# Query and gating-unit input blocks computed as two seven-product pairs, their rows kept in DRAM

## The chip, the cores and the metric

One core of a Trainium2 chip runs the kernel. Its engines are TensorE (PE: matmuls, with PEld for the loading of its stationary operand), VectorE (DVE), ScalarE (ACT), GpSimd (POOL) and SyncE (SP); each takes its instructions in order. SP, ACT and POOL also issue the DMA transfers. The metric is device time in microseconds, the median of several runs. Three runs of the kernel before took 1492.59, 1493.43 and 1494.11 us.

## The reference

Two layers of a bidirectional encoder over 512 positions and 2048 features, everything in float32:

```python
def hybrid_layer(x, ...):
    h = rms_norm(x, norm_w)
    proj = jnp.einsum('bsd,de->bse', h, w_in)          # 2048 -> 6144 columns
    q, k, v, g_attn, c_in, c_b, c_c, g_conv, s_u, s_v, g_sgu = split(proj)
    o_attn = attention_branch(q, k, v, ...)            # per-head rms norm of q and k, axial rope,
                                                       # 8 query heads on 2 key/value heads
    o_conv = short_conv_branch(c_in, c_b, c_c, conv_w) # c_b * conv3(c_c * c_in)
    o_sgu = sgu_branch(s_u, s_v, ...)                  # gelu(u) * (W_s norm(gelu(v)) + b), 4 groups of 128
    mixed = concatenate([rms_norm(o) * silu(gate) for each branch])
    return x + jnp.einsum('bse,ed->bsd', mixed, w_out) # 2048 -> 2048
```

A last RMS norm follows the second layer.

## The kernel before, in words

The input projection has twelve blocks of 512 columns. Block 0 holds k and v, 1 and 2 the queries, 3 and 4 the attention's gate, 5 to 8 the convolution, 9 to 11 the gating unit's v, its u and its gate. Each block is one `product` (L201): 16 feature tiles of 128, four accumulators of 128x512. Float32 accuracy comes from splitting each operand into a high and a low part and summing three matmuls, so that a product has 16 x 4 x 3 = 192 matmuls. Weights arrive in pairs of tiles (`load_pair`, L75, three buffers `wr`, issued by SP); `weight_parts` (L195) makes the two parts: ACT casts the high one (`wH`, L98), DVE subtracts to get the low one (`wL`, L99), five buffers each. The RMS norm's per-feature weight is multiplied into x when x is split; its per-position factor `rx` is applied when a product's rows leave the accumulators.

A layer runs block 0, then blocks 1 and 2 (`qblock`, L388: rows scaled by `rx`, `rope_rows` at L295 for norm and rope, then a 32x32 block transpose on DVE with a trip through DRAM to turn them), then attention per head (`scores` L347, `values` L372) with the convolution's blocks 5 to 8. Then come block 9 and the norm of gelu(v) (L453 to L467: gelu, square, reduce, four scaled multiplies, split into `vnH` and `vnL`), block 10, the gating matmuls (L477 to L479), block 11, and the gates 3 and 4 (`gates`, L500).

The output projection is already done in fewer multiplications: two calls of `pair` (L588), each of which computes two 512-column blocks as one 2x2 block product in seven products of 48 matmuls instead of eight (Winograd's form of Strassen's scheme). Its operands are halves and sums of halves of the mixed rows (A11 to N4), its weights running sums (X, Y), some of them formed by accumulating DMA transfers on POOL's queue (L596, L632). Between the layers, rows of the result go to DRAM (`Rows`), and `arrive` (L726) reads them back transposed, scales them on ACT (L733) and splits them into the next layer's operands.

A tile scheduler sets the order of instructions on each engine from the program's order, its dependences and the number of buffers per tag; a buffer comes free when its last reader is done. `mA`, `kv`, `qa`, `qb` and `o` are tags of large tiles, `t`, `qr` and `p` tags of 128x512 tiles with four buffers each. `acc` (4), `sc` (3) and `ps` (1) are the eight accumulator banks.

Of the kernel before, what the change touches and what calls it, by code (L numbers as in the profile page):

```python
# [8 lines left out]
F32 = mybir.dt.float32  # L9
# [5 lines left out]
P = 128  # L15
D = 2048
S = 512
# [16 lines left out]
def trunk_kernel(ctx: ExitStack, tc: tile.TileContext, xT, xn, win, wout, wcols, convw, qkw, sgun,  # L34
# [15 lines left out]
    def nm(s):  # L50
        uid[0] += 1
        return f"{s}_{uid[0]}"
# [84 lines left out]
    class Transposer:  # L137
# [27 lines left out]
        def get(self, t):  # L165
            return self.e[:, t]

    def by_block(ap):
        return ap.rearrange("p (s a i) -> p s a i", a=4, i=32)

# [50 lines left out]

    sqx = Squares()

    xraw = [big.tile([P, 4, S], F32, tag="mA", name=f"xraw{i}", bufs=4) for i in range(4)]
    first = []

    def load_x(k, n):
# [33 lines left out]
    for l in range(L):  # L261
# [6 lines left out]
        else:  # L268
            acc = product(win[l, 0], False, kps=kps, then=late)
            Rx = broadcast_x(rx)  # L270

        cos = lay.tile([P, ST, HD], F32, tag="swH", name=nm("cos"))
        sin = lay.tile([P, ST, HD], F32, tag="swL", name=nm("sin"))
        nc.sync.dma_start(out=cos, in_=rope[:, 0])
# [8 lines left out]
        nc.sync.dma_start(out=sb, in_=sgub[l])  # L283


        def rows_out(ps, st, n, on_act):
            q = T("qr")
            c = rx[:, st:st + 1]
            if on_act:
                nc.scalar.activation(q[:, :n], ps[:, :n], AF.Copy, scale=c)  # L290
            else:
                nc.vector.tensor_scalar(out=q[:, :n], in0=ps[:, :n], scalar1=c, scalar2=None, op0=ALU.mult)
            return q

        def rope_rows(q, st, nh, w):  # L295
            n = nh * HD
            qv = q[:, :n]
            t2 = T()
            nc.scalar.activation(t2[:, :n], qv, AF.Square)
# [3 lines left out]
            rq = rstd(ss, nh, 1.0 / HD)  # L303
            t1 = T()
# [16 lines left out]
        def transposed(rows, n, dst):  # L321
            tr = Transposer(n, "mA", 4)
            for st in range(ST):
                tr.put(st, rows[st][:, :n * HD])
            tr.move()
            for h in range(n):
                split(by_block(dst[h][0]), by_block(dst[h][1]), tr.get(h))
            return dst

        krows, vt = [], []  # L330
        for st in range(ST):
            krows.append(rows_out(acc[st], st, 256, True))
            v = T()
            nc.vector.tensor_scalar(out=v[:, :256], in0=acc[st][:, 256:], scalar1=rx[:, st:st + 1], scalar2=None,
                                    op0=ALU.mult)
            vt.append(v)
        vT = big.tile([P, ST, S], F32R, tag="kv", name=nm("vT"), bufs=2)
        kTt = big.tile([P, 2 * NKV, S], F32R, tag="kv", name=nm("kT"), bufs=2)
        for st in range(ST):
            split(vT[:, st, :256], vT[:, st, 256:], vt[st][:, :256])  # L340
        for st in range(ST):
            rope_rows(krows[st], st, NKV, qw[:, 1])
        kT = transposed(krows, NKV, [(kTt[:, 2 * h], kTt[:, 2 * h + 1]) for h in range(NKV)])

        oat = []

# [38 lines left out]
            nc.scalar.copy(o, po)  # L385
            oat.append(o)

        def qblock(b):  # L388
            acc = product(win[l, 1 + b], False)
            rows = [rows_out(acc[st], st, S, st % 2 == 0) for st in range(ST)]  # L390
            for st in range(ST):
                rope_rows(rows[st], st, 4, qw[:, 0])
            tag = "qa" if b == 0 else "qb"
            return transposed(rows, 4, [[big.tile([P, S], F32R, tag=tag, name=nm(tag), bufs=8) for _ in range(2)]
                                        for _ in range(4)])

        qs = qblock(0) + qblock(1)
        prev = None
        for h in range(NQ):
            cur = scores(h, qs[h])  # L400
# [70 lines left out]
        for st in range(ST):  # L471
# [17 lines left out]
        acc = product(win[l, 11], False)  # L489
        tr = Transposer(4, "mA", 4)  # L490
        for st in range(ST):
            g = T("qr")
            nc.scalar.activation(g, acc[st], AF.Silu, scale=rx[:, st:st + 1])
# [190 lines left out]
        if not last:  # L684
            out_rows = {}
            xH, xL = [None] * KT, [None] * KT

            class Rows:


                def __init__(self, spare):
                    self.spare = spare
                    self.m = dram.tile([P, 4, ST, 4 * 32], F32, tag="mv", name=nm("mv"), bufs=6)
                    self.got = 0

                def put(self, st, rows):
                    if self.got == 0 and self.spare:
                        self.both = big.tile([P, 2, 4, 2, 4, 32], F32, tag="mA", name=nm("blk"), bufs=4)
                    if self.got % 2 == 0:
                        if self.spare:  # L700
                            self.d = self.both[:, self.got // 2]
                        else:
                            self.d = big.tile([P, 4, 2, 4, 32], F32, tag="o", name=nm("blk"), bufs=2)
                    nc.vector.transpose(out=self.d[:, :, st % 2].rearrange("p b t i -> p t b i"),
                                        in_=rows.rearrange("p (t b j) -> p t b j", b=4, j=32))
                    self.got += 1
                    if self.got % 2 == 0:
                        nc.scalar.dma_start(out=self.m[:, :, st - 1:st + 1],
                                            in_=self.d.rearrange("p b s t i -> p b s (t i)"))

                def back(self):
                    e = big.tile([P, 4, ST * 4 * 32], F32, tag="mA", name=nm("rearr"), bufs=4)
                    mv = self.m.rearrange("(a j) b s f -> b j a (s f)", a=4)
                    for b in range(4):
                        nc.sync.dma_start(out=e[32 * b:32 * b + 32], in_=mv[b])
                    return e.rearrange("p a (s t i) -> p t s a i", s=ST, t=4)

            def complete(b, st, junk):
                c = C[b, st]
                squares(b, st, junk)  # L720
                nc.sync.dma_start(out=x1d[b, st], in_=c)
                if b not in out_rows:
                    out_rows[b] = Rows(b == 0)
                out_rows[b].put(st, c)

            def arrive(b):  # L726
                e_ = out_rows[b].back()
# [121 lines left out]
```

## Time and profile before

| | |
|---|---|
| median of three runs | 1493.43 us (1492.59 to 1494.11) |
| profiled execution | 1494.47 us, span 1492.7 us |
| mean granted clock of TensorE | 0.992 of full speed |
| PE busy | 1462.6 us (98%), 6422 matmuls |
| DVE busy | 972.4 us (65%), 1854 instructions |
| ACT busy | 681.3 us (46%), 1253 instructions |
| POOL busy | 112.3 us (8%), 120 instructions |
| HBM read, written | 186.96 MB, 36.70 MB |

The span is the time from the first to the last instruction of the profiled execution; the rest of its time lies around it. Matmuls are pipelined, so that one has a duration of about 0.39 us in the rows while the next starts 0.23 us after it. The page's chain of work that ended last gives PE 90% of the span and DMA 6%.

### The profile page before, as it was taken

To read this page: it belongs to the slowest core of one execution; us is meant where nothing else is said; L and a number is where in the kernel's file an instruction comes from. 1 tells how busy PE (TensorE), PEld (TensorE's weight loads), DVE (VectorE), ACT (ScalarE), POOL (GpSimd) and SP (SyncE) were. 2 spreads that over 40 slices of the span, in tenths; PEclk is the share of its full clock that TensorE was granted. 3 is DMA by queue.
4 is the path that set the end of the run, shared out by engine and by line. 5 is a ranking of instruction groups with operands and counts; after the bars stand their busy time and mean duration, and the time that the engine had idled before them with its cause. 6 is when DMAs were issued, how large, how long until landed. Compare 5 with 4: busy or idle time off the path is not lost.

```text
span 1492.7 us, 18358 instructions
## 1 busy us (share of the span) xinstructions
PE 1462.6 (98%) x6422; PEld 1205.5 (81%) x6422; DVE 972.4 (65%) x1854; ACT 681.3 (46%) x1253; POOL 112.3 (8%) x120
## 2 busy tenths in 40 slices
PE   9999999999999999997989999999999999999997
PEld 7888888888888888876868888888888888888785
DVE  7657898645553467875846578986455534678676
ACT  7333365533332446555643343565333334465553
POOL 0110000000011001111000100000000110011110
PEclk9999999999999999998999999999999999999999
DMA  7344577623337634697664345776232376346963
GB/s 277 102 114 141 181 217 225 184 86 99 92 101 210 202 96 101 141 328 179 178 165 128 113 141 173 222 217 192 85 99 92 99 209 194 106 100 143 251 139 130
DMA packets 78909, 233.25 MB, mean 156 GB/s; under 512 B 9184, under 2 KB 14560, under 8 KB 76000
## 3 DMA queue, kind: packets, MB, share of 16 engines
q1 hardware_dynamic: 65088, 202.68, 43.8%
q0 software_dynamic: 9216, 25.17, 9.3%
q10 hardware_dynamic: 4512, 4.23, 0.8%
q8 instruction: 50, 0.82, 0.2%
q14 instruction: 43, 0.35, 0.1%
HBM read 186.96 MB, written 36.70 MB: 150 GB/s over the span
## 4 chain that ended last, share of the span: by engine, by line
PE 90%; DMA 6%; DVE 1%; ACT 1%; SPq 1%; issue 0%; ACTq 0%; POOLq 0%
PE acc L218 59%; PE sc L218 9%; PE acc L611 3%; PE acc L612 3%; PE acc L613 3%; PE sc L613 2%; PE sc L611 2%; PE sc L612 2%; DMA mv<-blk 2%; DMA rearr<-mv 2%; PE ps L381 1%; PE ps L382 1%; PE ps L383 1%; PE sc L357 1%; PE sc L355 1%; PE sc L356 1%
## 5 line engine op out<-in xcount | busy, mean ns | idle before, releaser
L99 DVE TENSOR_TENSOR wL<-wr,wH 128x512 fp32r<-128x512 f32 x448 | 304.0, 685 | 355.1 <-ACT wH L98 325.5
L98 ACT CAST wH<-wr 128x512 fp32r<-128x512 f32 x448 | 275.9, 621 | 532.6 <-PE acc L218 390.6
L218 PE MATMUL acc<-x,wH 128*128 128x512 f32 x1408 | 436.8, 389 | 0.4 <-DVE qr L420 0.4
L218 PE MATMUL acc<-wH,x 128*128 128x512 f32 x1280 | 393.0, 391 | 7.6 <-ACT wH L98 7.6
L218 PEld LDWEIGHTS acc<-x,wH 128*128 128x128 f32 x1408 | 264.2, 188 | 55.6 <-DVE qr L420 0.8
L218 PEld LDWEIGHTS acc<-wH,x 128*128 128x128 f32 x1280 | 240.9, 189 | 59.6 <-ACT wH L98 9.5
L218 PE MATMUL acc<-x,wL 128*128 128x512 f32 x704 | 273.2, 389 | 0.0
L218 PE MATMUL acc<-wL,x 128*128 128x512 f32 x640 | 244.2, 390 | 0.0
L218 PEld LDWEIGHTS acc<-x,wL 128*128 128x128 f32 x704 | 132.2, 188 | 27.4
L218 PEld LDWEIGHTS acc<-wL,x 128*128 128x128 f32 x640 | 120.4, 188 | 25.4 <-DVE wL L99 0.4
L611 PE MATMUL acc<-wH,n 128*128 128x512 f32 x192 | 75.9, 395 | 7.5 <-ACT wH L98 7.5
L105 POOL TENSOR_TENSOR s<-s,negh 128x4 f32<-128x4 f32 (+2 forms) x44 | 52.3, 1190 | 369.7 <-DVE s L103 364.2
L218 PE MATMUL sc<-wH,x 128*128 128x512 f32 x256 | 78.8, 389 | 0.0
L612 PE MATMUL acc<-wH,n 128*128 128x512 f32 x192 | 75.7, 394 | 0.0
L99 DVE TENSOR_TENSOR wL<-wx,wH 128x512 fp32r<-128x512 f32 x88 | 57.7, 684 | 24.2 <-ACT wH L98 18.7
L98 ACT CAST wH<-wx 128x512 fp32r<-128x512 f32 x88 | 52.8, 619 | 36.9 <-PE acc L218 11.9
L364 ACT ACTIVATE p<-sc,sa 128x512 f32<-128x512 f32 x64 | 44.1, 689 | 54.4 <-DVE sa L361 37.2
L613 PE MATMUL acc<-wL,n 128*128 128x512 f32 x192 | 66.1, 394 | 0.0
L218 PEld LDWEIGHTS sc<-wH,x 128*128 128x128 f32 x256 | 48.1, 188 | 10.0
L218 PE MATMUL sc<-wL,x 128*128 128x512 f32 x128 | 49.8, 389 | 0.0
L98 ACT CAST wH<-wy 128x512 fp32r<-128x512 f32 x64 | 38.9, 622 | 23.2 <-PE sc L612 12.8
L611 PEld LDWEIGHTS acc<-wH,n 128*128 128x128 f32 x192 | 36.6, 191 | 15.6 <-ACT wH L98 7.9
(231 smaller groups left out, 1963.7 us busy)
## 6 DMA issues: line engine op xcount, KB each, us to landing
wr<-in_win SPq DMA_DIRECT2D x191, 512.0 KB, 3.6
rearr<-mv SPq DMA_DIRECT2D x104, 256.0 KB, 5.4
mv<-blk SPq DMA_DIRECT2D x22, 1024.0 KB, 4.7
wr<-in_wout SPq DMA_DIRECT2D x32, 512.0 KB, 5.4
wy<-in_wout SPq DMA_DIRECT2D x16, 512.0 KB, 5.2
wy<-in_wout POOLq DMA_DIRECT2D x16, 512.0 KB, 9.2
wx<-in_wout SPq DMA_DIRECT2D x16, 512.0 KB, 8.3
wx<-wy POOLq DMA_DIRECT2D x16, 512.0 KB, 5.0
```

What stands on the lines that cost most here:

```text
L98: nc.scalar.copy(H, src)
L99: nc.vector.tensor_tensor(out=Lo, in0=src, in1=f32(H), op=ALU.subtract)
L105: nc.gpsimd.tensor_tensor(out=r, in0=v, in1=negh[:, :n], op=ALU.pow)
L218: nc.tensor.matmul(acc[e], a, b, start=(kp == kps[0] and j == 0 and i == 0), stop=(kp == kps[-1] and j == 1 and i == 2))
L355: nc.tensor.matmul(sc, qH[:, ss], kH, start=True, stop=False)
L356: nc.tensor.matmul(sc, qH[:, ss], kL, start=False, stop=False)
L357: nc.tensor.matmul(sc, qL[:, ss], kH, start=False, stop=True)
L364: nc.scalar.activation(p, sc, AF.Exp, scale=SCALE, bias=nm_, accum_out=su)
L381: nc.tensor.matmul(po, a, pH[:, t], start=(t == 0), stop=False)
L611: nc.tensor.matmul(bank[t], a, H, start=(k == 0 and p not in (6, 4)), stop=False, skip_group_check=True)
L612: nc.tensor.matmul(bank[t], c, H, start=False, stop=False, skip_group_check=True)
L613: nc.tensor.matmul(bank[t], a, Lo, start=False, stop=(k == 7), skip_group_check=True)
```

## The change

Blocks 1 and 2, and blocks 10 and 11, are each computed as a pair of seven products (`early_pair`), right behind block 0 and ahead of attention. The order is p = 1, 7, 5, 3, 6, 2, 4. Operands are the halves of the existing xH and xL, and four new sums of halves (E1 to E4) that `difference` builds for eight pairs of feature tiles: two scaled copies on ACT, four half-width adds on DVE, two splits. Weight sums are kept in four X tiles (tag `kv`, two buffers); at p=7 each weight tile gets X added to it in turn: X += w on DVE, then w += the second block's lower half by an accumulating transfer on POOL. For its last quarter w is a pair of 128x512 tiles (`spare`) instead of a `wr` buffer. q rows are roped with `rx` folded in and go through `Rows` to DRAM, as do the k rows; v rows, gelu(u) and silu(gate) go to DRAM as they are, and are read back where they are used. In layer 0 two of the raw x tiles move to the tag `kv`. In layer 1 `difference` works on rows that `arrive` kept, two of which are read again from DRAM. In the output projection the x1d stores go from SP's queue to POOL's, and the two `arrive` calls come behind p=5 and p=2 instead of p=3 and p=6.

```diff
+        def difference(k, i, lo, hi, shape=lambda ap: ap):
+            t0, t8 = T(), T()
+            nc.scalar.activation(shape(t0), lo, AF.Copy, scale=wc[:, 0, k:k + 1])
+            nc.scalar.activation(shape(t8), hi, AF.Copy, scale=wc[:, 0, 8 + k:9 + k])
+            nc.vector.tensor_tensor(out=t8[:, HALF:], in0=t0[:, HALF:], in1=t8[:, HALF:], op=ALU.subtract)
...
+            for (a, b), src, (h, lo_) in (((E2, E3), t0, tiles_[:2]), ((E4, E1), t8, tiles_[2:])):
+                split(h, lo_, src)
...
+        def early_pair(b0, b1, tags, complete):
+            s0, s1 = win[l, b0], win[l, b1]
+            wx = [big.tile([P, 2, 2, S], F32, tag="kv", name=nm("wx"), bufs=2) for _ in range(2)]
+            X = [wx[i // 2][:, i % 2] for i in range(4)]
+            for i in range(4):
+                nc.sync.dma_start(out=X[i], in_=s0[i])
...
+            for p in (1, 7, 5, 3, 6, 2, 4):
...
+                    if p == 7:
+                        if i < 3:
+                            w = load_pair(s1[i])
+                            nc.vector.tensor_tensor(out=X[i], in0=X[i], in1=w, op=ALU.add)
+                            nc.gpsimd.dma_start(out=w, in_=s1[4 + i], accum_op=ALU.add)
+                            w = [w[:, 0], w[:, 1]]
+                        else:
+                            w = spare
+                            for j in range(2):
+                                nc.sync.dma_start(out=w[j], in_=s1[i][:, j])
+                                nc.vector.tensor_tensor(out=X[i][:, j], in0=X[i][:, j], in1=w[j], op=ALU.add)
+                                nc.gpsimd.dma_start(out=w[j], in_=s1[4 + i][:, j], accum_op=ALU.add)
+                    elif p in (3, 2):
+                        w = load_pair((s1 if p == 3 else s0)[4 + i])
+                        nc.vector.tensor_tensor(out=X[i], in0=X[i], in1=w, op=ALU.add)
...
+        early_pair(1, 2, (("p", "p"), ("qr", "qr"), ("qr", "qr"), ("p", "sq")), q_rows)
+        early_pair(10, 11, (("qr", "qr"), ("qr", "qr"), ("p", "p"), ("p", "sq")), sgu_row)
...
-        acc = product(win[l, 10], False)
         gu = big.tile([P, ST, S], F32, tag="mA", name=nm("gu"), bufs=4)
-        for st in range(ST):
-            nc.scalar.activation(gu[:, st], acc[st], AF.Gelu, scale=rx[:, st:st + 1])
+        nc.sync.dma_start(out=gu, in_=sgu_rows[10])
...
-                nc.sync.dma_start(out=x1d[b, st], in_=c)
+                nc.gpsimd.dma_start(out=x1d[b, st], in_=c)
...
-            pair(2, 3, C, complete, False, {3: lambda: arrive(1), 6: lambda: arrive(0)})
+            pair(2, 3, C, complete, False, {5: lambda: arrive(1), 2: lambda: arrive(0)})
```

The order of the instructions moves in three places. On ACT, behind block 0 of layer 0, the kernel before has the next product's casts (wr_668 and later are weights of block 1):

```order
L98 CAST wH_534<-wr_482 128x512
L98 CAST wH_670<-wr_668 128x512
L98 CAST wH_686<-wr_668 128x512
L98 CAST wH_704<-wr_702 128x512
L98 CAST wH_720<-wr_702 128x512
L290 ACTIVATE qr_562<-acc_164,rc_501 128x256
```

The changed kernel has there the copies from the raw x tiles and the casts of E parts (e), and then the first casts of X weights (wx_764):

```order
L306 ACTIVATE t_640<-xraw_141,wc_144 128x512
L307 ACTIVATE t_641<-xraw_143,wc_144 128x512
L98 CAST e_635<-t_627 128x512
L98 CAST e_635<-t_628 128x512
L306 ACTIVATE t_653<-xraw_141,wc_144 128x512
L98 CAST e_648<-t_640 128x512
L307 ACTIVATE t_654<-xraw_143,wc_144 128x512
L98 CAST e_648<-t_641 128x512
L349 ACTIVATE t_692<-qr_680 128x256
L98 CAST wH_784<-wx_764 128x512
```

The last copies from xraw now stand ahead of the first cast of the next product. On DVE, in the same stretch of layer 0, the kernel before ropes q rows (qr) between the low parts of one product's weights (L307 to L319 are steps of `rope_rows`, L145 the transpose):

```order
L99 TENSOR_TENSOR wL_1119<-wr_1116,wH_1118 128x512
L307 SCALAR_TENSOR_TENSOR t_956<-qr_940,s_954,qw_554 128x128 x4
L301 TENSOR_REDUCE s_967<-t_965 128x4
L313 TENSOR_TENSOR t_948<-t_956,sin_551 128x8x32 x2
L103 TENSOR_SCALAR s_969<-s_967 128x4
L317 TENSOR_TENSOR t_956<-t_956,cos_550 128x512
L319 TENSOR_TENSOR qr_940<-t_956,t_948 128x512
```

The changed kernel has at p=7 of the q pair the low parts of accumulated weights (wr_914), the half-width adds of the last quarter (wx_765 with the spare tiles qr_772 and qr_773), and between them the K rows' rope and transposes (qr_683, qr_686):

```order
L99 TENSOR_TENSOR wL_919<-wr_914,wH_918 128x512
L103 TENSOR_SCALAR s_730<-s_728 128x2
L371 TENSOR_TENSOR t_717<-t_717,cos_666 128x256
L99 TENSOR_TENSOR wL_929<-wr_914,wH_928 128x512
L433 TENSOR_TENSOR wx_765<-wx_765,qr_772 128x512
L373 TENSOR_TENSOR qr_683<-t_717,t_709 128x256
L361 SCALAR_TENSOR_TENSOR t_734<-qr_686,s_732,qw_670 128x128 x2
L184 STREAM_TRANSPOSE blk_707<-qr_683 128x2x4x32
```

The adds into X and the low parts that depend on transfers now share the queue with the rope. On PE, ahead of the gating matmuls of layer 0, the kernel before has 206 matmuls between the last one of block 9 and the first of the gating: those of block 10 and some of another product. The last of them and the first of the gating are:

```order
L218 MATMUL acc_4097<-wH_4119,x_108 128x512
L218 MATMUL acc_4097<-wH_4119,x_124 128x512
L218 MATMUL acc_4097<-wL_4120,x_108 128x512
L218 MATMUL acc_4098<-wH_4119,x_108 128x512
L218 MATMUL acc_4098<-wH_4119,x_124 128x512
L477 MATMUL sc_4049<-vnH_3702,swH_3422 128x512
L478 MATMUL sc_4049<-vnL_3703,swH_3422 128x512
```

The changed kernel has 15 there, of the gates' product (L247):

```order
L247 MATMUL acc_4735<-x_110,wH_4788 128x512
L247 MATMUL acc_4735<-x_126,wH_4788 128x512
L247 MATMUL acc_4735<-x_110,wL_4789 128x512
L247 MATMUL acc_4735<-x_111,wH_4806 128x512
L247 MATMUL acc_4735<-x_127,wH_4806 128x512
L247 MATMUL acc_4735<-x_111,wL_4807 128x512
L631 MATMUL sc_4659<-vnH_4591,swH_4311 128x512
L631 MATMUL sc_4664<-vnH_4591,swH_4311 128x512
```

Block 10's product no longer stands between block 9 and the gating. In all the order has 6188 rows on PE instead of 6380, 2002 on DVE instead of 1712, and 1301 on ACT instead of 1105.

## Rows read from the trace of the kernel before

**Rows 1.** Section 1 of the page: busy time, share, instructions
```profile
PE 1462.6 (98%) x6422; PEld 1205.5 (81%) x6422; DVE 972.4 (65%) x1854; ACT 681.3 (46%) x1253; POOL 112.3 (8%) x120
```

**Rows 2.** Chain that ended last, a long product: start, length, what
```profile
536.52 44.88 PE acc L218 x198
```

**Rows 3.** PE's waits: line, waited for: total us, times, longest
```profile
PE acc L611 <- ACT wH L98: 7.9, 2, 7.5
PE acc L218 <- ACT wH L98: 7.6, 3, 6.3
```

**Rows 4.** Chain that ended last, change of layers
```profile
664.80 15.24 DMA mv<-blk
...
680.94 0.43 SPq L715
...
681.41 5.68 DMA rearr<-mv
...
745.42 7.67 DMA rearr<-mv
```

**Rows 5.** By stretch: length, PE, PEld, DVE, ACT, POOL busy, PEclk, DMA, GB/s
```profile
583.00:643.00 60.00, 60.00 (x265) 49.43 (x265) 53.62 (x86) 36.38 (x68) 11.42 (x13) 1.00 0.65 156
680.00:690.00 10.00, 2.86 (x13) 2.04 (x11) 0.00 (x0) 2.80 (x5) 0.00 (x0) 0.75 0.48 108
690.00:694.00 4.00, 3.69 (x9) 2.92 (x10) 3.25 (x5) 3.30 (x7) 1.68 (x2) 0.50 0.73 167
756.00:760.00 4.00, 3.69 (x9) 2.91 (x10) 3.71 (x7) 4.00 (x10) 0.00 (x0) 0.50 0.17 66
```

**Rows 6.** DVE in order of time, two stretches: start, us, line, operation
```profile
411.68 1.13 DVE L465 SCALAR_TENSOR_TENSOR qr<-qr,s,sn 128x128 f32<-128x128 f32 x4
...
590.25 0.42 DVE L529 TENSOR_TENSOR t<-o,t 128x256 f32<-128x256 f32 x1
590.59 0.69 DVE L99 TENSOR_TENSOR lA<-o,hA 128x512 fp32r<-128x512 f32 x1
591.19 1.29 DVE L99 TENSOR_TENSOR wL<-wy,wH 128x512 fp32r<-128x512 f32 x2
...
595.14 1.22 DVE L634 TENSOR_TENSOR wy<-wx,wr 128x1024 f32<-128x1024 f32 x1
596.27 0.69 DVE L99 TENSOR_TENSOR n<-t,n 128x512 fp32r<-128x512 f32 x1
```

**Rows 7.** Groups by form: busy, mean ns | idle before
```profile
L98 ACT CAST wH<-wr 128x512 fp32r<-128x512 f32 x448 | 275.9, 621 | 532.6 <-PE acc L218 390.6 <-PE sc L218 60.3 <-PE acc L612 23.2
L733 ACT ACTIVATE t<-rearr,wc 128x512 f32<-128x512 f32 x16 | 10.6, 712 | 27.7 <-DMA rearr<-mv 27.4 <-DVE x L99 0.4
```

**Rows 8.** DMA issues: count, KB each, median us to landing
```profile
wr<-in_win SPq DMA_DIRECT2D x191, 512.0 KB, 3.6
...
wy<-in_wout POOLq DMA_DIRECT2D x16, 512.0 KB, 9.2
wx<-in_wout SPq DMA_DIRECT2D x16, 512.0 KB, 8.3
...
c<-in_xn POOLq DMA_DIRECT2D x10, 256.0 KB, 6.6
...
p<-in_xn POOLq DMA_DIRECT2D x6, 256.0 KB, 4.2
```

**Rows 9.** Line L596 alone: POOL's accumulating transfers of 512 KB
```profile
DMA to landing us min/median/max: 7.9/9.2/13.7
```

**Rows 10.** Gating chain: last matmul of block 9, last split of vnL
```profile
404.11 0.39 PE L218 MATMUL acc<-wL,x 128*128 128x512 f32 x1
...
422.06 0.69 DVE L99 TENSOR_TENSOR vnL<-qr,vnH 128x512 fp32r<-128x512 f32 x1
```

More of the change, by code (lines that the diff above doesn't have):

```diff
@@ L166, in get, with __init__, put, back @@
             return self.e[:, t]
+    class Rows:
+        def __init__(self, n, spare):
+            self.n, self.spare, self.got = n, spare, 0
+            self.m = dram.tile([P, 4, ST, n * 32], F32, tag="rows", name=nm("rows"), bufs=8)
+        def put(self, st, rows):
+            n = self.n
+            if self.got == 0 and self.spare:
+                self.both = big.tile([P, 2, 4, 2, n, 32], F32, tag="mA", name=nm("blk"), bufs=4)
+            if self.got % 2 == 0:
+                if self.spare:
+                    self.d = self.both[:, self.got // 2]
+                else:
+                    self.d = big.tile([P, 4, 2, n, 32], F32, tag="o", name=nm("blk"), bufs=2)
+            nc.vector.transpose(out=self.d[:, :, st % 2].rearrange("p b t i -> p t b i"),
+                                in_=rows.rearrange("p (t b j) -> p t b j", b=4, j=32))
+            self.got += 1
+            if self.got % 2 == 0:
+                nc.scalar.dma_start(out=self.m[:, :, st - 1:st + 1], in_=self.d.rearrange("p b s t i -> p b s (t i)"))
+        def back(self, tag, bufs):
+            e = big.tile([P, 4, ST * self.n * 32], F32, tag=tag, name=nm("rearr"), bufs=bufs)
+            mv = self.m.rearrange("(a j) b s f -> b j a (s f)", a=4)
+            for b in range(4):
+                nc.sync.dma_start(out=e[32 * b:32 * b + 32], in_=mv[b])
+            return e.rearrange("p a (s t i) -> p t s a i", s=ST, t=self.n)
     def by_block(ap):
@@ L222, in trunk_kernel @@
     sqx = Squares()
-    xraw = [big.tile([P, 4, S], F32, tag="mA", name=f"xraw{i}", bufs=4) for i in range(4)]
+    xraw = [big.tile([P, 4, S], F32, tag="kv" if i % 2 else "mA", name=f"xraw{i}", bufs=2 if i % 2 else 4)
+            for i in range(4)]
     first = []
@@ L283, in trunk_kernel, with rope_rows @@
         nc.sync.dma_start(out=sb, in_=sgub[l])
[L286 to L295, printed above, removed]
+        def rope_rows(q, st, nh, w, scale=None):
             n = nh * HD
@@ L303, in rope_rows @@
             rq = rstd(ss, nh, 1.0 / HD)
+            if scale is not None:
+                rs_ = small(nh)
+                nc.vector.tensor_scalar(out=rs_, in0=rq, scalar1=scale, scalar2=None, op0=ALU.mult)
+                rq = rs_
             t1 = T()
@@ L319, in rope_rows @@
             nc.vector.tensor_tensor(out=qv, in0=t1[:, :n], in1=t2[:, :n], op=ALU.add)
-        def transposed(rows, n, dst):
-            tr = Transposer(n, "mA", 4)
-            for st in range(ST):
[L324 to L330, printed above, removed]
-        for st in range(ST):
[L332 to L336, printed above, removed]
+        krows = Rows(NKV, False)
@@ new lines, in trunk_kernel @@
+        vrows = dram.tile([P, ST, 256], F32, tag="vrows", name=nm("vrows"), bufs=2)
+        kv_rows = []
+        for st in range(ST):
+            q = T("qr")
+            nc.scalar.activation(q, acc[st], AF.Copy, scale=rx[:, st:st + 1])
+            nc.sync.dma_start(out=vrows[:, st], in_=q[:, 256:])
+            kv_rows.append(q)
+        for st in range(ST):
+            rope_rows(kv_rows[st], st, NKV, qw[:, 1])
+            krows.put(st, kv_rows[st][:, :256])
+        operand_x = {1: [(xH[k][:, :HALF], xL[k][:, :HALF]) for k in range(8)],
+                     2: [(xH[8 + k][:, :HALF], xL[8 + k][:, :HALF]) for k in range(8)],
+                     4: [(xH[8 + k][:, HALF:], xL[8 + k][:, HALF:]) for k in range(8)],
+                     5: E1, 6: E2, 7: E3, 3: E4}
@@ new lines, in trunk_kernel, with q_rows, sgu_row @@
+        qrows = {b: Rows(4, False) for b in (1, 2)}
+        def q_rows(b, st, c):
+            rope_rows(c, st, 4, qw[:, 0], rx[:, st:st + 1])
+            qrows[b].put(st, c)
+        sgu_rows = {b: dram.tile([P, ST, S], F32, tag=f"sgu{b}", name=nm("sgu"), bufs=2) for b in (10, 11)}
+        def sgu_row(b, st, c):
+            nc.scalar.activation(c, c, AF.Gelu if b == 10 else AF.Silu, scale=rx[:, st:st + 1])
+            nc.sync.dma_start(out=sgu_rows[b][:, st], in_=c)
+        early_pair(1, 2, (("p", "p"), ("qr", "qr"), ("qr", "qr"), ("p", "sq")), q_rows)
@@ L337, in trunk_kernel @@
+        early_pair(10, 11, (("qr", "qr"), ("qr", "qr"), ("p", "p"), ("p", "sq")), sgu_row)
         vT = big.tile([P, ST, S], F32R, tag="kv", name=nm("vT"), bufs=2)
         kTt = big.tile([P, 2 * NKV, S], F32R, tag="kv", name=nm("kT"), bufs=2)
+        kT = [(kTt[:, 2 * h], kTt[:, 2 * h + 1]) for h in range(NKV)]
+        e_ = krows.back("mA", 4)
+        for h in range(NKV):
+            split(by_block(kT[h][0]), by_block(kT[h][1]), e_[:, h])
         for st in range(ST):
[L340 removed]
@@ L341, in trunk_kernel @@
-        for st in range(ST):
-            rope_rows(krows[st], st, NKV, qw[:, 1])
-        kT = transposed(krows, NKV, [(kTt[:, 2 * h], kTt[:, 2 * h + 1]) for h in range(NKV)])
+            v = T("qr")
+            nc.sync.dma_start(out=v[:, :256], in_=vrows[:, st])
+            split(vT[:, st, :256], vT[:, st, 256:], v[:, :256])
         oat = []
@@ L386, in values, with q_back @@
             oat.append(o)
[L388 to L397, printed above, removed]
+        def q_back(b):
+            e_ = qrows[b].back("mA", 4)
+            tag = "qa" if b == 1 else "qb"
+            got = []
+            for h in range(4):
+                H, Lo = [big.tile([P, S], F32R, tag=tag, name=nm(tag), bufs=8) for _ in range(2)]
+                split(by_block(H), by_block(Lo), e_[:, h])
+                got.append((H, Lo))
+            return got
+        qs = q_back(1) + q_back(2)
         prev = None
@@ L686, in trunk_kernel @@
             xH, xL = [None] * KT, [None] * KT
[L688 to L716, printed above, removed]
             def complete(b, st, junk):
```

89 lines of the change are left out of this document (83 added, 6 removed).

## The prediction, on record before the changed kernel ran

> **What bounds the kernel now.** I read the engines' shares first. PE is busy 98% of the span, DVE 65%, ACT 46% [rows 1]: as a whole the kernel is bound by the number of its matmuls. The chain of waits agrees: through a long product it holds nothing but matmuls, 198 of them in 44.88 us [rows 2], a pitch of 44.88/198 = 0.2267 us. So 192 matmuls, one product, are worth 43.5 us wherever PE is fed. Next come PE's waits, to see where it is not fed: two products wait for ACT's casts, longest 7.5 and 6.3 us [rows 3]. The chain shows both at the change of layers: ACT takes its work in order, and a copy of returned rows, whose transfer is under way, stands ahead of the casts [rows 4]. The table by stretch shows that PE pays twice for such a gap: it is busy 2.86 of the 10 us from 680, and in the 4 us behind each of the two gaps its granted clock is 0.50 (1.2 instead of 2.4 GHz) [rows 5]. The same table has the stage that resembles the new code most: from 583 to 643, in the first output pair, PE is busy all 60.00 us while DVE is busy 53.62 [rows 5]. DVE has little to spare there.
>
> **The change, part by part.** The sum is made against the profiled execution, 1494.47 us (span 1492.7); the median of the runs shown is 1.04 below.
>
> 1. *Matmuls.* Per layer four products of 192 become fourteen of 48: 96 fewer, 192 in all. **-43.5.**
>
> 2. *Seam behind the first product, layer 0.* The next product used to run straight on, its raw weights already loaded. Now the X weights go into the two buffers that hold xraw1 and xraw3, and these are read up to the last copies of `difference`: the order of ACT has all of those copies ahead of the first X cast. One `difference` costs DVE four half-width adds at a pitch of 0.34 and two splits at 0.60 [rows 6]: 2.5 us. It costs ACT two copies (712 ns) and two casts (621 ns) [rows 7], 2.7 at full length. There are four temporaries, so the copies of k=7 wait for the splits of k=5. The four evictions hold the start up to 5.6 us after the product; five more steps at 2.55 (between those two) bring the last copy to 18.4; an issue of 0.4 (the pitch of the issues in the chain, [rows 4], is of that size), a load of 3.6 [rows 8] and a cast of 0.62 [rows 7] follow, SP having the four vrows stores ahead of that load. **+23**, between 20 (first steps done beside the last matmuls) and 28 (loads at the pace of 6 to 9 us that transfers take under traffic, [rows 8]).
>
> 3. *The same seam in layer 1.* The order there leaves four of the eight differences for after the product, about 10 us less by the same steps. **+14**, 10 to 19.
>
> 4. *q pair, products 1 and 7.* At p=7 each weight tile is loaded, added to X on DVE (1.22 us), then gets a second block added by an accumulating transfer on POOL's queue, and only then is cast. The first add can run 4.4 us after product 1 begins, as it needs the splits of X[0]; its accumulation takes 9.2 us, 7.9 at least [rows 8, 9]. So the first cast comes at about 14 us, but product 1 ends at 48 x 0.2267 = 10.9. Then it builds up, by the order on DVE: wL_919 waits for an accumulation, and behind it stand the K rope rows and their transposes. These free the two `qr` tiles into which the last quarter of the weights is loaded; that load, its half-width add and its 256 KB accumulation (4.2 to 6.6, [rows 8]) follow one after the other. I work the end of product 7 out at 34 to 40 us behind the start of product 1, where 2 x 10.9 = 21.8 would do: 12 to 18, I take **+15 per layer, 30 in all**. Bounds: 9 (all accumulations at 7.9, rope rows early) and 19 per layer.
>  A rule bears on this. The row gives 9.2 us, 7.9 at least, for 512 KB accumulated from POOL's queue [rows 8, 9]. The Trainium skill, "DMA: Bandwidth & Descriptors", section "Anatomy of one DMA — SWDGE (gpsimd) path", fits such a transfer as about 2 us fixed plus its bytes over 436 GB/s: an estimate of 3.2 us for 512 KB. By that page each of the four pair starts would wait some 9 us less, and the sum would be near +57 instead of +92. The trace does not agree with the page for accumulating transfers, and the row decides.
>
> 5. *SGU pair.* The same start, but its two spare tiles are the slots of the q pair's c22 rows, which must first be roped and transposed: four scaled products (1.13 per four, [rows 6]), two half multiplies, a multiply, an add and a transpose, some 4.3 us of DVE for each tile. Over both pairs by the order DVE has 112 weight splits (0.60), 22 full adds (1.13 pitch, [rows 6]), about 22 eviction adds (0.6) and the rope of 8 q and 4 k tiles: about 155 us, against fourteen products of 48 matmuls, 152.4 us of PE. DVE is thus as long as PE, and what its waits for accumulations cost is not won back. End of product 7 at 36 to 43 instead of 21.8, +17.5; the later products, paced by DVE, +2.5. **+20 per layer, 40 in all**; 12 to 26 each.
>
> 6. *SGU gating.* Before, product 10 (206 matmuls) stood between product 9 and the gating matmuls, and hid the whole chain gelu, square, reduce, scale, split: product 9's last matmul is at 404.11, the last vnL split ends at 422.06 + 0.69 [rows 10], 18.4 us later, six weight splits interleaved. Now 15 matmuls of the gates (3.4 us) are all that the order has there; the gates cannot go further since three of their banks belong to the gating. 18.4 less about 2.4 (splits no longer between) less 3.4: **+12.5 per layer, 25 in all**; 8 to 16 each.
>
> 7. *Attention's start.* q and k rows come back through DRAM, 5.7 to 7.7 us for such a return [rows 4], mostly beside the convolution's products. **+4**, 0 to 8.
>
> 8. *Clock.* Eight new gaps of over 5 us; behind a gap the clock is 0.50 for a while, and the 3.69 us of PE in such a stretch [rows 5] would take about half at full clock: 1.9 each at most, not all gaps being long and unbroken. **+6**, 2 to 9.
>
> 9. *Change of layers.* arrive() comes two products later, the x1d stores leave SP's queue for POOL's, and the first of the two waits [rows 3] should shrink; but a split of product 2 now stands behind the copies of arrive(1). **-6**, -14 to +6.
>
> Sum: -43.5 + 23 + 14 + 30 + 40 + 25 + 4 + 6 - 6 = **+92.5**. 1494.5 + 92.5 - 1.0 = **1586 us**. All low ends together: -43.5 + 20 + 10 + 18 + 24 + 16 + 0 + 2 - 14 = +32.5, 1526. All high ends: -43.5 + 28 + 19 + 38 + 52 + 32 + 8 + 9 + 6 = +148.5, 1642.
>
> **The rivals.**
> *Pairs fed (milder).* For it: the first output pair has the same accumulations, and PE is busy 60.00 of 60 us [rows 5]. Against it: there the Y tiles have buffers of their own and are issued before product 1, while here each addition waits for X's splits and a tile to free. Items 4 and 5 at nothing: -43.5 + 23 + 14 + 25 + 4 + 6 - 6 = +22.5, **1516 us**.
> *DVE keeps ahead (other side).* All new waits are DVE's queue seen from elsewhere. If DVE ran ahead of PE through the pairs, and at the seams and in the gating did only what nothing precedes, these would cost 18 and 9, below the bounds above, and 8 per layer in gating, the pairs nothing: -43.5 + 27 + 16 - 6 = -6.5, **1487 us**. It decides once all new waits together stay under 49.5 us; I count 142. For it speaks only DVE's share, 65% [rows 1]; against it that the share is an average, and the new work stands in one stretch.
> *Starvation spreads (worse).* Attention and the convolution, interleaved on the same queues, lose as well, beyond item 7: all high ends, **1642 us**.
> That the change does not do what it says can be left out: the matmuls are counted in the order.
>
> **How the numbers follow.** Forecast 0.72, pairs fed 0.12, DVE keeps ahead 0.09, starvation 0.07. A measurement of this kernel can tell a change of about 0.2% (3 us) from none. Of the other side's 0.09, 0.07 falls to faster and 0.02 to the same; all else is slower: 0.91. The forecast's own range is 1540 to 1630. The range for 8 in 10 takes in the milder case: 1510 to 1630. It leaves out the other side (0.09), starvation (0.07) and some of the forecast's edges.
>
> **What would show it.** In the trace of the changed kernel: PE waiting some 20 us for ACT's first cast of an X tile behind the first product, and 10 to 15 in layer 1 (items 2, 3); four stretches at product 7 with PE waiting for casts of tiles whose accumulation has just landed, DVE waiting in order ahead of rope rows (4, 5); PE waiting for the vnH and vnL splits with gate matmuls on either side (6); a granted clock of 0.50 behind each (8). Wrong would be: PE without gaps in the pairs, accumulations of 512 KB well under 7.9 us, or a seam under 15 us. PE's idle time should be about 130 us more than before; if it is under 50, the other side holds.

## The result, and the profile after

The changed kernel takes 1579.97 us (median of four runs, 1579.04 to 1580.52) where the kernel before takes 1493.12: a ratio of 1.058, 95% interval 1.0562 to 1.0598. Forecast were 1586 us. The profiled execution took 1579.53 us, 85.1 more than that of before.

First the engines' shares of the changed kernel, which answer to [rows 1] (engine, busy us, share, instructions):

```profile
PE 1443.7 (92%) x6230; PEld 1178.9 (75%) x6230; DVE 1150.3 (73%) x2146; ACT 784.9 (50%) x1437; POOL 147.2 (9%) x156
```

PE has 192 matmuls less, as counted, but its share falls from 98% to 92%: it waits. DVE has 178 us more to do, most of it beside PE's work. PE's waits, which answer to [rows 3] (line, waited for: total us, times, longest):

```profile
PE acc L447 <- ACT wH L98: 48.2, 11, 10.8
PE sc L447 <- ACT wH L98: 37.6, 2, 22.2
PE sc L631 <- ACT vnH L98: 19.4, 2, 9.7
PE acc L247 <- ACT wH L98: 4.6, 5, 2.6
...
PE acc L764 <- ACT wH L98: 0.4, 1, 0.4
```

The first three rows are the change. Two waits of 37.6 in all are the seams, one per layer (product 1 writes to the `sc` banks). The 48.2 are the waits inside the pairs, in the `acc` banks of product 7. The 19.4 are the gating. Nothing like them stands in the kernel before, whose two largest waits, 7.9 and 7.6 in all, have shrunk to 0.4 and 4.6 in the same places (L764 and L247).

The seam of layer 0, rows of ACT, SP's queue and PE in order of time (start, length; in brackets the idle time before and what ended it):

```profile
70.57 0.72 ACT L306 ACTIVATE t<-xraw,wc 128x512 f32<-128x512 f32 x1 [0.53 <-DVE e L99]
71.32 1.93 SPq L397 DMA_DIRECT2D wx<-in_win  x4
71.70 0.72 ACT L307 ACTIVATE t<-xraw,wc 128x512 f32<-128x512 f32 x1
...
74.93 1.14 ACT L98 CAST wH<-wx 128x512 fp32r<-128x512 f32 x2 [1.68 <-DMA wx<-in_win]
...
75.60 0.80 PE L447 MATMUL sc<-wH,x 128*128 128x512 f32 x1 [22.21 <-ACT wH L98]
```

The load of the first X tiles starts 0.03 us after the last copy from xraw1 has ended: the buffer is the bond, as item 2 has it. Landing and cast follow, and PE starts 22.2 us late. But the cast stands behind the same copies in ACT's order too, and waited for the load only the 1.68 us in its bracket (1.37 in layer 1): with this order an earlier load alone would have gained no more.

Product 7 of the query pair in layer 0, all engines, its last quarter only (qr are the spare tiles and the K rows whose slots they take):

```profile
92.01 0.33 SPq L432 DMA_DIRECT2D qr<-in_win  x1
...
96.14 0.68 DVE L433 TENSOR_TENSOR wx<-wx,qr 128x512 f32<-128x512 f32 x1
...
97.42 0.93 POOL L434 DMA_DIRECT2D qr<-in_win  x1 [1.25 <-DVE qr L373]
97.60 0.43 DVE L184 STREAM_TRANSPOSE blk<-qr 128x256 f32<-128x256 f32 x1
...
98.06 0.33 SPq L432 DMA_DIRECT2D qr<-in_win  x1
...
103.59 0.62 ACT L98 CAST wH<-qr 128x512 fp32r<-128x512 f32 x1 [5.99 <-DMA qr<-in_win]
103.72 0.69 DVE L433 TENSOR_TENSOR wx<-wx,qr 128x512 f32<-128x512 f32 x1 [2.95 <-DMA qr<-in_win]
104.26 0.80 PE L447 MATMUL acc<-wH,e 128*128 128x512 f32 x1 [6.70 <-ACT wH L98]
105.02 0.91 POOL L434 DMA_DIRECT2D qr<-in_win  x1 [5.25 <-DVE t L367]
...
109.12 0.62 ACT L98 CAST wH<-qr 128x512 fp32r<-128x512 f32 x1 [4.91 <-DMA qr<-in_win]
...
109.79 0.50 PE L447 MATMUL acc<-wH,e 128*128 128x512 f32 x1 [2.60 <-ACT wH L98]
```

Read it backwards: PE waits for a cast, the cast for an accumulation, the accumulation for an add (X takes w in before w may change; it is X that gets the tile added, not the tile X), the add for a load, the load for the transpose of a K row (97.60) whose tile it takes. The first three quarters cost nothing here: between 86.7 and 97.2 PE has no gap. Their accumulations were quicker than I took them to be. Transfers of the changed kernel by issue, which answer to [rows 8, 9] (count, KB each, median us to landing):

```profile
wy<-in_wout POOLq DMA_DIRECT2D x16, 512.0 KB, 8.8
...
wr<-in_win POOLq DMA_DIRECT2D x12, 512.0 KB, 5.7
...
qr<-in_win POOLq DMA_DIRECT2D x8, 256.0 KB, 4.2
```

The output pairs' accumulations still take 8.8; the new ones of the same size take 5.7 (5.3 to 7.1). The trace points at traffic: where the output pair issues four of them within about 6 us (L749, from 553.1 and from 1335.1), the first takes 5.9 and 5.8, the fourth 12.5 and 11.3. In the kernel before the page had a second row of 512 KB accumulations, from one tile into another (L632, 4.5 at least), which the prediction did not weigh:

```profile
wx<-wy POOLq DMA_DIRECT2D x16, 512.0 KB, 5.0
```

The gating of layer 0, last split of vnL and first gating matmul, which answer to [rows 10]:

```profile
544.58 0.69 DVE L99 TENSOR_TENSOR vnL<-qr,vnH 128x512 fp32r<-128x512 f32 x1 [0.69 <-ACT vnH L98]
...
544.60 1.65 PE L631 MATMUL sc<-vnH,swH 128*128 128x512 f32 x3 [9.71 <-ACT vnH L98]
```

And the clock behind the seam, by stretch (length, PE, PEld, DVE, ACT, POOL busy, granted clock, DMA share, GB/s), which answers to [rows 5]:

```profile
54.00:75.00 21.00, 0.00 (x0) 0.00 (x0) 18.78 (x42) 16.85 (x30) 0.24 (x1) 0.55 0.16 53
75.50:80.00 4.50, 4.40 (x10) 3.47 (x11) 4.42 (x9) 4.01 (x9) 0.00 (x0) 0.50 0.59 237
```

PE does ten matmuls in 4.5 us behind its idle stretch, at a clock of 0.50.

### The profile page after: what moved, and what is told of

Its sections match the earlier page's. It is cut to its first block, busy times and chain, and to the rows that moved or that the text cites. A ratio compares the mean times of both kernels' runs of the same rounds, so it can differ in the third digit from the quotient of the medians.

```text
span 1577.7 us, 18856 instructions
## 1 busy us (share of the span) xinstructions
PE 1443.7 (92%) x6230; PEld 1178.9 (75%) x6230; DVE 1150.3 (73%) x2146; ACT 784.9 (50%) x1437; POOL 147.2 (9%) x156
## 4 chain that ended last, share of the span: by engine, by line
PE 71%; DMA 12%; DVE 8%; ACT 4%; issue 2%; POOL 1%; SPq 1%; ACTq 0%; POOLq 0%; DVEq 0%
PE acc L247 35%; PE acc L766 3%; PE acc L765 3%; PE acc L764 3%; DMA qr<-in_win 3%; PE acc L447 2%; PE acc L449 2%; PE acc L450 2%; DMA rearr<-rows 2%; PE sc L247 2%; PE sc L764 2%; PE sc L765 2%; PE sc L766 2%; DMA wr<-in_win 2%; PE sc L447 2%
## 5 line engine op out<-in xcount | busy, mean ns | idle before, releaser
L99 DVE TENSOR_TENSOR wL<-wr,wH 128x512 fp32r<-128x512 f32 x408 | 274.1, 685 | 200.1 <-ACT wH L98 189.1
L247 PE MATMUL acc<-x,wH 128*128 128x512 f32 x1344 | 416.4, 389 | 0.6 <-DVE qr L576 0.6
L247 PEld LDWEIGHTS acc<-x,wH 128*128 128x128 f32 x1344 | 252.2, 188 | 53.8 <-DVE qr L576 1.0
L247 PE MATMUL acc<-x,wL 128*128 128x512 f32 x672 | 260.3, 389 | 2.5 <-DVE wL L99 2.5
L98 ACT CAST wH<-wx 128x512 fp32r<-128x512 f32 x216 | 129.9, 619 | 101.7 <-PE acc L449 21.7
L99 DVE TENSOR_TENSOR wL<-wx,wH 128x512 fp32r<-128x512 f32 x216 | 142.5, 684 | 33.9 <-ACT wH L98 27.2
L247 PE MATMUL acc<-wH,x 128*128 128x512 f32 x512 | 155.9, 392 | 5.1 <-ACT wH L98 4.6
L247 PEld LDWEIGHTS acc<-x,wL 128*128 128x128 f32 x672 | 126.1, 188 | 29.5 <-DVE wL L99 3.3
L247 PEld LDWEIGHTS acc<-wH,x 128*128 128x128 f32 x512 | 95.6, 188 | 27.3 <-ACT wH L98 6.8
L447 PE MATMUL acc<-wH,e 128*128 128x512 f32 x128 | 56.6, 442 | 48.4 <-ACT wH L98 48.2
L247 PE MATMUL acc<-wL,x 128*128 128x512 f32 x256 | 95.1, 390 | 0.0
L764 PE MATMUL acc<-wH,n 128*128 128x512 f32 x192 | 74.7, 389 | 0.0
L447 PE MATMUL sc<-wH,x 128*128 128x512 f32 x64 | 27.2, 424 | 37.6 <-ACT wH L98 37.6
L247 PE MATMUL sc<-x,wH 128*128 128x512 f32 x192 | 58.4, 391 | 0.0
L247 PEld LDWEIGHTS acc<-wL,x 128*128 128x128 f32 x256 | 48.0, 188 | 10.3 <-DVE wL L99 0.4
```

Of the source, the lines that this page charges most:

```text
L98: nc.scalar.copy(H, src)
L99: nc.vector.tensor_tensor(out=Lo, in0=src, in1=f32(H), op=ALU.subtract)
L247: nc.tensor.matmul(acc[e], a, b, start=(kp == kps[0] and j == 0 and i == 0), stop=(kp == kps[-1] and j == 1 and i == 2))
L447: nc.tensor.matmul(bank[t], a, H, start=(k == 0 and p not in (6, 4)), stop=False, skip_group_check=True)
L764: nc.tensor.matmul(bank[t], a, H, start=(k == 0 and p not in (6, 4)), stop=False, skip_group_check=True)
```

## The experiments

All times are medians; the kernel before ran beside each at 1493.2 to 1493.5 us. "Gap" is the time between the starts of two matmuls beyond the pitch of 0.227 us, counted from 0.5 us upwards.

**The last quarter without its spare tiles.**

```diff
-                        if i < 3:
                             w = load_pair(s1[i])
...
-                            w = spare
-                            for j in range(2):
-                                nc.sync.dma_start(out=w[j], in_=s1[i][:, j])
```

> The last quarter of product 7's weights goes through a wr buffer like the other three, not through two qr tiles. Theory S (the four stalls at product 7, 51 us of PE gaps in the changed kernel, are the chain of the last quarter: a qr tile freed by the rope, then load, half-width add, accumulation): the wr buffer is free after the first quarter's split, near 88.5 in the first pair, and the quarter is cast near 100.3 instead of 104.3 and 109.1; gaps fall from 51 to about 16 us, the time to about 1541 us. Rival D (DVE is as long as PE in the pairs and its work is the same): time within 5 us of 1580.

Measured 1567.2 us, ratio 1.0493 (1.0477 to 1.0508). Gaps at product 7 fell from 51 to 33 us, not to 16, and the time lies between the theory's 1541 and the rival's 1575 or more: half right. DVE, ACT and POOL in the first pair show why:

```profile
94.70 0.69 DVE L99 TENSOR_TENSOR wL<-wr,wH 128x512 fp32r<-128x512 f32 x1 [1.58 <-ACT wH L98]
...
95.72 0.68 DVE L99 TENSOR_TENSOR wL<-wr,wH 128x512 fp32r<-128x512 f32 x1
...
96.32 1.22 DVE L425 TENSOR_TENSOR wx<-wx,wr 128x1024 f32<-128x1024 f32 x1
...
98.14 0.93 POOL L426 DMA_DIRECT2D wr<-in_win  x1 [1.78 <-DVE qr L373]
...
103.49 1.14 ACT L98 CAST wH<-wr 128x512 fp32r<-128x512 f32 x2 [5.17 <-DMA wr<-in_win]
```

The last quarter's add stands in DVE's order behind low parts of the third quarter, which wait for that quarter's own accumulation. Taking away the tile left the queue.

**No accumulation.**

```diff
-                            nc.gpsimd.dma_start(out=w, in_=s1[4 + i], accum_op=ALU.add)
...
-                                nc.gpsimd.dma_start(out=w[j], in_=s1[4 + i][:, j], accum_op=ALU.add)
```

> Leaves out the accumulating transfers of product 7 (its weights are the first summand alone). Theory S: the last quarter still waits for its qr tiles and its loads; gaps at product 7 about 27 of 51 us, time about 1553 us. Rival A (the accumulations alone make the stalls): gaps near 0, about 1525 us. Rival D (DVE): no change, 1575 to 1580 us.

Measured 1545.3 us (1.0341, 1.0322 to 1.0359). PE's waits in this kernel:

```profile
PE sc L445 <- ACT wH L98: 37.0, 2, 22.2
PE sc L629 <- ACT vnH L98: 19.4, 2, 9.7
PE acc L445 <- ACT wH L98: 14.7, 7, 4.1
```

Seams and gating stay; 48.2 becomes 14.7. So of the waits inside the pairs some 33 us hang on accumulations and 15 on the tiles and loads alone. The expectation of 27 of 51 left gave the tiles too much.

**The last quarter not summed.**

```diff
+                            w2 = load_pair(s1[4 + i])
+                            w = [w[:, 0], w[:, 1], w2[:, 0], w2[:, 1]]
```

> The last quarter of product 7 is not summed: its two summands are loaded into wr buffers and multiplied one after the other, 12 matmuls more in each pair (2.7 us each, 10.9 in all), no spare tiles, nothing left out. Theory S: gaps at product 7 near 0; 1580 - 51 - 6 (half clock behind the gaps) + 11 = about 1534 us. Rival D: two weight splits more on DVE in each pair, the gaps come back in the later products; 1570 us or more.

Measured 1558.4 us (1.0433, 1.0416 to 1.045), between the two. No gap of more than 1.8 us is left at product 7, but the gating pair has new ones of 1.6 and 6.0 us in each layer, later on. DVE and PE at the second:

```profile
228.09 0.68 DVE L455 TENSOR_TENSOR qr<-acc,qr 128x512 f32<-128x512 f32 x1
...
228.83 0.80 PE L443 MATMUL acc<-wH,x 128*128 128x512 f32 x1 [5.84 <-DVE qr L455]
```

Product 2 waits for the bank of product 5, whose eviction add stands on DVE behind the rope of the query rows. Rival D had a part in it.

**Only the query pair.**

```diff
-        early_pair(10, 11, (("qr", "qr"), ("qr", "qr"), ("p", "p"), ("p", "sq")), sgu_row)
...
+        acc = product(win[l, 10], False)
```

> Only the query blocks are a pair; blocks 10 and 11 are plain products at their old places. Theory: 96 matmuls come back (+21.8), the gating pair's gaps (-32) and the gating gaps (-23) go, with half clock behind them (-8): about 1539 us, seams and the query pair's gaps unchanged. Rival (DVE's backlog from the rope of the query rows passes to whatever comes next, here attention): 1550 us or more.

Measured 1536.6 us (1.0288, 1.0271 to 1.0305): as expected. The wait for the vn parts is gone from the list, the seams stay at 36.4. The gating pair, with the cover that it took from the gating counted in, costs 43 us more than it saves.

**Banks for the first gate product.**

```diff
+        banks.update(seq=["acc"] * 4, at=0)
         ev0 = gates(0)
```

> The first gate product gets the four acc banks instead of the three sc banks and one acc bank; the order then has about 128 matmuls instead of 15 between block 9 and the gating. Theory (the gating chain of 18 us has no cover): gaps of 11.4 us in each layer fall to 1 or less, half clock behind them goes (about 2 each), the second gate product waits some 2 us for its banks: about 1557 us. Rival (the chain gets later with the gates' weight splits between its steps, and the same wait comes after those matmuls): 1572 us or more.

Measured 1561.2 us (1.0448, 1.043 to 1.0467). Both gating gaps are gone; 2.3 and 1.9 us are new in front of the second gate product. The gating wait was lack of cover, and the banks kept the cover away.

**Block 9 as cover for the seam.**

```diff
+        acc = product(win[l, 9], False)
+        vrow9 = dram.tile([P, ST, S], F32, tag="sgu9", name=nm("sgu"), bufs=2)
+
         E1, E2, E3, E4 = [[None] * 8 for _ in range(4)]
```

> Block 9 moves from behind the convolution to directly behind block 0; its gelu rows go to DRAM and are read back for the gating chain, nothing left out. Theory (seams and gating chain are work without cover; a product of 43.5 us hides them): the gaps of 22.4 and 15.5 us behind block 0 fall to 2 or less, the gating gaps of 11.4 each to 2 or less, the K rope lies beside block 9 so that the query pair's gaps fall from 19 to about 6, half clock behind them goes: 1580 - 36 - 21 - 13 - 8 = about 1502 us. Rival (the differences are DVE and ACT time that only moves into product 1 and 7): 1540 us or more.

Measured 1543.7 us (1.0334, 1.0318 to 1.035). The seams are gone (no gap above 0.7 us behind block 0), the query pair's gaps fell from 19.1 to 2.4. But the gating got worse, 12.1 and 4.8 us in each layer:

```profile
539.62 2.72 DVE L572 SCALAR_TENSOR_TENSOR oc<-oc,wc,ps 128x512 f32<-128x512 f32 x4 [0.42 <-PE ps L129]
...
551.70 0.69 DVE L99 TENSOR_TENSOR vnL<-qr,vnH 128x512 fp32r<-128x512 f32 x1 [0.68 <-ACT vnH L98]
551.72 1.65 PE L637 MATMUL sc<-vnH,swH 128*128 128x512 f32 x3 [11.92 <-ACT vnH L98]
```

So the time came out in the rival's range (1540 or more), but not for the rival's reason: the difference work did vanish behind block 9, and the expected end of the gating gaps failed. Having the rows early does not start the chain early: its squares still ran only from 534 on (L621), amid the normalisations (L572) in DVE's order, and block 9 no longer lay between them and the gating.

**Both.** cover9 with the last quarter not summed:

> cover9 and split_last together, nothing left out. If the two are independent: 1580 - 78 (cover9, as expected there) and the gating pair's 32 to about 15 (its banks still wait for qr tiles that the rope holds), 11 us of more matmuls: about 1492 us. If cover9 already takes away what split_last gains, 1505 us.

Measured 1541.8 us (1.0315, 1.0296 to 1.0335): no better than cover9 and far from both expected times, since some 25 us (10.9 of matmuls, 14.2 of gaps in the gating pair) take the place of the stalls, and the gating's 34 remain.

**Chain earlier, other spare tiles.**

```diff
+            if j == 3:
+                chain_ = gating_chain()
             acc = product(win[l, 5 + j], True)
...
-            spare = two(tags[1])
+            spare = two(tags[1] if b0 == 1 else ("t", "t"))
```

> cover9 with two edits: the gating chain is written ahead of the last convolution product instead of behind the normalisations, and the gating pair's spare tiles are t tiles, not qr tiles; nothing left out. Theory: the gating gaps (12.1 and 4.8 in each layer in cover9) go because the chain has a product beside it; the gating pair's gaps fall from 15.3 in each layer to about 3, because its last quarter no longer waits for the roped rows: 1543.7 - 34 - 24 - 8 = about 1478 us. Rival (that pair waits because DVE is as long as PE there): its gaps stay above 10 in each layer, 1495 us or more.

Measured 1535.3 us (1.0278, 1.0265 to 1.0291). The gating gaps are gone. The gating pair's gaps went the other way, from 15.3 to over 28 us in each layer. Rows of SP's queue, DVE and ACT:

```profile
211.78 0.70 DVE L184 STREAM_TRANSPOSE blk<-p 128x512 f32<-128x512 f32 x1
...
216.28 0.80 SPq L439 DMA_DIRECT2D t<-in_win  x2
216.53 0.70 DVE L184 STREAM_TRANSPOSE blk<-p 128x512 f32<-128x512 f32 x1
...
224.46 0.62 ACT L98 CAST wH<-t 128x512 fp32r<-128x512 f32 x1 [12.17 <-DMA t<-in_win]
```

The rope's own temporaries are t tiles: the spare loads, which in the changed kernel start behind the third and fourth of the eight roped rows, now start behind the rope of the seventh. The same chain, moved the wrong way, shows that it is the chain; the time is in the rival's range, but both3, next, speaks against its reason.

**The same without spare tiles in the gating pair.**

```diff
-                        if i < 3:
+                        if i < 3 or b0 == 10:
```

> both2, but the gating pair's last quarter goes through a wr buffer as in no_spare, so that no tile the rope holds stands in its way; nothing left out. Theory (in both2 the t tiles came free only behind the eighth roped row, which made the gaps of 27 us): the gaps fall to those of no_spare's gating pair, 9 in the first layer and 8 in the second: 1535.3 - 56.8 + 17 = about 1496 us, level with the kernel before. Rival (DVE's own length in the pairs sets the end, whatever the tiles): 1520 us or more.

Measured 1491.6 us (0.9984, 0.9976 to 0.9993): the waits at product 7 fall from 57.2 to 16.2, and both pairs together come level with the kernel before. DVE's length (77% of the span, the highest share of all versions) did not set the end.

**One part alone, in the kernel before.**

```diff
-                nc.sync.dma_start(out=x1d[b, st], in_=c)
+                nc.gpsimd.dma_start(out=x1d[b, st], in_=c)
...
-            pair(2, 3, C, complete, False, {3: lambda: arrive(1), 6: lambda: arrive(0)})
+            pair(2, 3, C, complete, False, {5: lambda: arrive(1), 2: lambda: arrive(0)})
```

> The kernel before with only the change of layers of the changed one: x1d stores on POOL's queue, arrive behind p=5 and p=2. Theory: the two gaps at the change of layers fall from 14 to about 6 us: 1485 us. Rival (what shortened them is the other tag of the returned rows, kv, not the order): 1493 us or more.

Measured 1487.5 us (0.9958, 0.9944 to 0.9972): 0.4% faster. PE's waits, beside [rows 3]:

```profile
PE acc L611 <- ACT wH L98: 4.3, 2, 3.8
PE sc L611 <- ACT wH L98: 4.0, 3, 2.5
PE acc L218 <- ACT wH L98: 3.8, 5, 1.5
```

The two gaps at the change of layers fell from 14.1 to 5.7 us; the middle row was 1.4 before, and has a new gap of 2.7 us inside the second output pair. Since both3 has this change of layers too, its 1491.6 is 4 us slower than this run: the two pairs as such still cost more than they save.

**The query pair with cover.** q_only with block 11 behind block 0:

> q_only with block 11 directly behind block 0, its silu rows to DRAM and back, block 10 left between block 9 and the gating; nothing left out. Theory (the seam and the query pair's wait for rope are one lack of cover): from q_only's 1536.6 the seams' 36.7 us go, the query pair's gaps fall from 20 to about 3 as in cover9, half clock behind them goes (about 7): about 1476 us, faster than the kernel before. Rival (the 87 us of block 11 were needed as cover between the gating and the output projection): the wait comes back there, 1490 us or more.

Measured 1480.7 us (0.9912, 0.9898 to 0.9927), faster than both kernels. PE's waits begin with

```profile
PE acc L247 <- ACT wH L98: 4.4, 4, 3.2
PE sc L774 <- DVE wL L99: 2.9, 2, 2.4
```

and no seam, pair or gating stands among the large ones. Against the run above with the same change of layers it saves 8.7 us of span: 21.8 of matmuls, less 13.0 of gaps (none above 3.4) and half clock that it has more.

**Matmuls of ones in the seam.**

```diff
+            for _ in range(84):
+                nc.tensor.matmul(pd.rearrange("p (a b) -> p a b", b=P), onesr,
+                                 onesr.unsqueeze(1).broadcast_to([P, ST, P]), start=True, stop=True)
```

> The changed kernel with 84 matmuls of ones into an unused bank in the seam of layer 0, 19 us of PE work that nothing uses. Theory: the seam's end does not move (it is DVE's and the load's), and the granted clock stays at 1.00 behind it, so that product 1 ends about 2 us earlier; the whole about 2 us shorter. Rival (the half clock belongs to the first matmuls of a bank or of an operand): clock 0.50 behind the seam all the same.

One run: 1584.9 us. By stretch, beside the rows of the changed kernel above:

```profile
54.00:75.00 21.00, 19.34 (x84) 15.69 (x84) 18.80 (x42) 16.96 (x30) 0.40 (x1) 1.00 0.17 57
75.00:80.00 5.00, 4.65 (x20) 3.86 (x21) 4.67 (x9) 5.00 (x11) 0.31 (x1) 1.00 0.60 236
```

Twenty matmuls in 5 us instead of ten in 4.5: the clock stays at 1.00 when PE has been busy. But nothing was won. Product 1 ended earlier, and product 7 then waited 3.0 us near 93 where it had not waited, for accumulations that were not earlier. The half clock of the seam had been hidden by the stall behind it. Why the whole came out 5 us longer, in one run, is not settled. Matmul by matmul it is 1.3 us behind the changed kernel at the query pair's end, 2.8 where the first product beside attention begins (328), 6.4 in the second output pair (720), 8.8 behind the change of layers (803) and 5.4 near the end: no one place has it.

## Why the prediction was right, point by point

The direction and size held because most terms did. Terms in us, forecast and measured (gaps of the two profiled executions; half clock counted as the part of matmuls' spacing above the pitch, so that items 4 and 5 hold none of it):

| item | forecast | measured |
|---|---|---|
| 1 matmuls | -43.5 | -43.5 |
| 2 seam, layer 0 | +23 | +22.4 |
| 3 seam, layer 1 | +14 | +15.5 |
| 4 query pairs | +30 | +19.1 |
| 5 gating pairs | +40 | +31.9 |
| 6 gating | +25 | +22.8 |
| 7 attention's start | +4 | +4.2 |
| 8 clock | +6 | about +16.6 |
| 9 change of layers | -6 | about -7.4 |
| small gaps | - | +3.5 |
| sum | +92.5 | +85.1 |

Items 2 and 3 were right in mechanism and place: the casts come behind the last copies, by ACT's order and by the buffer, and cover9 removed both. What a buffer of its own for X would give was not tried. Item 6 was right, the reason about banks included. Item 9 was right, and its part alone makes the kernel before 0.4% faster.

Items 4 and 5 have one mis-sized term: an accumulation of 512 KB at 9.2 us. It was 5.7 in the new pairs. The row that I took it from was measured in the output pairs, where they still took 8.8; why they are quicker here was not tested. So the step "the first cast comes at about 14 us, but product 1 ends at 10.9" failed: in the first pair the cast came at 11.0, and product 1, part of it at half clock and four matmuls of product 7 already among it, ended at 14.5. The first three quarters were ready, but for one gap of 1.3 to 1.9 us in each of the other three pairs, and the last one, behind the rope, made the stall; with the K rope out of its way (cover9) the query pairs' gaps are 2.4. Accumulations "well under 7.9 us" were one of the prediction's own signs of being wrong, and this one came. PE's idle time also fell short: 104 us more than before, not 130.

The end of product 7, counted from the start of product 1, was nearly met all the same: 37.6 and 36.7 us in the query pairs (forecast 34 to 40), 44.1 and 43.2 in the gating pairs (36 to 43). But beside the gaps there stands in it half clock, which the prediction had in item 8, and 1 to 3 us of neighbouring products' matmuls.

The rule of the Trainium skill that spoke against the row ("DMA: Bandwidth & Descriptors", "Anatomy of one DMA — SWDGE (gpsimd) path") gives an estimate of 3.2 us. The runs do not show that either: of the new ones the shortest was 5.3 us, and where the sum by that rule was near +57, the time came out at +85. The "+2.5" in item 5 for later products paced by DVE did not come: behind product 7 no gap is counted in any of the four pairs. (both3 has 0.9 and 1.6 us there.)

Item 8 was too small by ten. It counted eight gaps and took 0.75 us for each, less than its upper figure of 1.9, since not all would be long and unbroken. The trace has twelve stretches at half clock where the kernel before has two, since three of the four stalls at product 7 come in two pieces; and a stretch costs about 1.8 us (106 matmuls at 0.2 us each). At 1.9 the eight alone would have made 15. Items 4 and 5 were 19 too high; item 8 was 11 too low, and 3.5 of small gaps stood in no item. That these partly cancel is luck.

The rival "pairs fed" was refuted by product 7's waits, and "DVE keeps ahead" by the seams; "starvation spreads" did not come, as attention and the convolution lost only the 4.2 of item 7. both3 shows under what conditions the time of "DVE keeps ahead" (1487) would nearly come: with a cover at the seam, the gating chain earlier and the tile chain broken, 1491.6 us.

## What to carry to other kernels

Fewer matmuls pay only where operands are ready: here 43.5 us of products were saved, and 112 us of waits came at the places where the removed or moved products had been the cover. Ask of every buffer that a new stage takes who reads it last, and of every helper tile which row must leave it first; both kinds of large stall had at their head a buffer that came free late, though at the seam ACT's order stood 1.7 us behind it, and at product 7 taking the tile away won only 18 of 51 us. Take a transfer's price from a stretch that resembles the new one, and keep the bound of its shortest record open downwards.

## What the runs showed of the hardware

Accumulating transfers of one size and queue took 5.7 us in one stage and 8.8 us in another of the same execution. Behind twelve idle stretches of PE in the changed kernel the granted clock was 0.50 (1.2 of 2.4 GHz) for six to fourteen matmuls, once only from the fifth matmul on; behind a thirteenth, of 2.8 us at the change of layers, it stayed at 1.00. With PE kept busy through the seam it stayed at 1.00 too; in the one run of it, giving that clock back gained nothing, as the next wait was a transfer's.
